# Gate and value products of a feed-forward as 2x2 blocks with seven block products

## The chip, the cores and the metric

One core of one Trainium2 chip runs the whole program once. The metric is the device time of that execution in microseconds; the kernel before has a median of 2009.08 us over three executions (2008.69 to 2012.46).

## The reference

Four layers over 512 tokens of width 1024, in float32. The first two layers are a mixer (three kinds of attention) and a gated feed-forward; the last two are a recurrent layer ("even") and a gated linear attention layer ("odd"). The change touches the feed-forward of the first two layers alone:

```python
D_MODEL, SEQ, DEPTH = 1024, 512, 2
D_FF = -(-(8 * D_MODEL) // (3 * 256)) * 256     # 2816
for l in range(DEPTH):
    ...
    hn = rms_norm(h, ffn_norm[l])
    gu = hn @ w_gate_up[l]
    h = h + (jax.nn.silu(gu[..., :D_FF]) * gu[..., D_FF:]) @ w_down[l]
```

## The kernel before, in words

Activations lie feature-major: eight tiles of 128 features x 512 tokens. A matmul's float32 operands are each split in two, hi (rounded to the matmul's format) and lo (what is left), and a product is three matmuls into one bank, hi x hi, hi x lo, lo x hi (`mm3`). Weights arrive as units of 128x1024 (512 KB): `wunit` (L316) loads one into a `wr` tile, ScalarE writes `wh`, VectorE writes `wl` as the difference. There are two `wr`, three `wh` and three `wl` buffers; this work has a raised priority, so that it runs ahead of what is next in the program. The rest is ordered by a static planner by priority and program order, each engine then running its queue in order. `evac` takes a product out of PSUM with a multiplication, also at raised priority.

`ffn` (L1276) first calls `prenorm` (L558), which makes the split activations `xs` (`xh`, `xl`) of h times the norm's weight, and `RB`, the reciprocal root mean square of each token spread over all partitions (`RH` is half of it). Then it goes over NF = 22 blocks of 128 hidden columns in groups of 8, 8 and 6. For each block: a gate product (`dense_fm`: 8 k-tiles x 3 = 24 matmuls of 512 columns), taken out as `fz` times RB, tanh on ScalarE into `fth`, a scalar_tensor_tensor on VectorE, then the value product (24 more), taken out as `fth` times RH, their product, and its split into `fah`, `fal`. This is called the gate stage below. Behind each group comes the down stage: for eight outputs a unit of `wd` and 24 (or 18) matmuls over the group's `fah`, `fal`, and an addition into h. PSUM has four tags (pd, pt, pr, pa) of two banks each. Elementwise helpers are `tt` (L285), `stt` (L303), `act` (L306), and the matmul is L366; so lines in the trace are mostly those of helpers, and names of tiles tell operations apart. GpSimd does nothing in the feed-forward. Its few sums stand in the first norm (`acc`) and in the "seam" between the even and the odd layer (`RH`, `sq`, 256 columns).

Of the kernel before, what the change touches and what calls it, by code (L numbers as in the profile page):

```python
# [5 lines left out]
F32 = mybir.dt.float32  # L6
F32R = mybir.dt.float32r
BF16 = mybir.dt.bfloat16
I32 = mybir.dt.int32
AF = mybir.ActivationFunctionType  # L10
ALU = mybir.AluOpType
# [4 lines left out]
P = 128  # L16
T = 512
# [8 lines left out]
UNIT = 1024  # L26
# [12 lines left out]
WPRI, SMPRI, EPRI, CPRI, SPRI = 300, 0, 200, 500, 600  # L39
# [3 lines left out]

WEAVE, VAT, QAT, VDELAY, QAHEAD, RPOST = 1.9, (2, 6, 10, 14), 6, 1, 3, 20
MSCB, MOB, DB0, DB1, DB2 = ("pa", "pr", "pa", "pr"), "pd", ["pd", "pt"], ["pd"], ["pd"]

EARLY, SEAM, LATE, AH2, AH3 = (3, 5), (3, 1, 5, 5, 1), 2, -300, -250

# [170 lines left out]
class _Kernel:  # L219
# [1053 lines left out]
            self.add(self.h[m], ps, self.h[m])  # L1273


    def ffn(self, l):  # L1276
        self.dbanks = ["pd", "pt", "pr"]
        xs, rT, RB, RH = self.prenorm(f"ffn_norm{l}", half=True)
        for k0 in range(0, NF, 8):
            n = min(8, NF - k0)  # L1280
            acts = []
            for m in range(k0, k0 + n):
                pg = self.dense_fm(self.a["wgu"][l, 2 * m], xs)
                z = self.t("fz", "Z")
                self.evac(z, pg, RB)
                th = self.t("fth", "Z")
                self.act(th, z, AF.Tanh, scale=0.5)
                self.stt(z, th, 1.0, z, ALU.add, ALU.mult)
                pu = self.dense_fm(self.a["wgu"][l, 2 * m + 1], xs)
                self.evac(th, pu, RH)  # L1290
                self.mul(z, z, th)
                acts.append(self.split(z, "fa", "F"))
            for m in range(KD):
                ps = self.pd()
                self.dense(ps, self.wunit(self.a["wd"][l, m, :, k0 * P:(k0 + n) * P], n * P), acts)
                self.add(self.h[m], ps, self.h[m])
        if l == 0:
            self.h_kept = self.dr.tile([D, T], F32, tag="hk", name="hk")
        for m in range(KD):
            if l == 0:  # L1300
                self.nc.sync.dma_start(out=self.h_kept[m * P:(m + 1) * P, :], in_=self.h[m])
# [496 lines left out]
    def run(self):  # L1798
        self.setup()
        for l in range(L2):  # L1800
            with self.phase("attn", R=26, M=15, I=2):
                self.attn(l)
            with self.phase("ffn", F=40, Z=8):
                self.ffn(l)
        self.softplus()
        with self.phase("even", A=16, B=16, D=7, U=3, G=7, W=2):
            self.even()
        with self.phase("odd", Q=8, V=8, G=8, L=8, QS=8, K=8, S=3):
            self.odd()
# [42 lines left out]
```

## Time and profile before

| | us |
|---|---|
| median of three executions | 2009.08 |
| the profiled execution: time | 2010.3 |
| the profiled execution: span, first to last instruction | 2008.5 |
| TensorE, VectorE, ScalarE, GpSimd busy in the span | 1972.3, 1274.5, 808.1, 68.9 |
| granted TensorE clock, mean share | 0.998 |
| a gate stage of 8 blocks, a down stage behind it | 87.0, 43.5 |

The time is the span and 1.8 us around it. Matmuls are pipelined: the duration of one is its latency, and what it costs is the distance from its start to the next one's. VectorE's operations overlap a little in the same way. A busy engine is the bound of a stage only if the others wait for it there.

### The profile page before, as it was taken

What the parts mean: (1) busy time and instruction counts of PE and PEld (TensorE: products, weight loads), DVE (VectorE), ACT (ScalarE), POOL (GpSimd) and SP (SyncE); (2) the same over time, 40 slices, a digit from 0 to 9 for tenths busy, and PEclk for the clock granted to TensorE, in tenths of its full rate; (3) what the DMA queues carried; (4) which work ended last, traced back from release to release, by engine and by line L of the source; (5) the groups of instructions that cost most, each with busy time, mean ns of one, the idle gap of its engine ahead of it and who ended that gap; (6) DMA issues with size and microseconds to landing.
All of it is one profiled execution on the core that took longest, in us unless ns stands there. A gap on an engine that the chain in (4) does not pass through costs nothing.

```text
span 2008.5 us, 25747 instructions
## 1 busy us (share of the span) xinstructions
PE 1972.3 (98%) x10016; PEld 1582.8 (79%) x10016; DVE 1274.5 (63%) x2367; ACT 808.1 (40%) x1323; POOL 68.9 (3%) x116
## 2 busy tenths in 40 slices
PE   8999999999999999999999999999999999999998
PEld 5777678888888877766788888888888888888886
DVE  7874665544535688647555354458988884389665
ACT  6523553322223444336433222234545453347242
POOL 3100000000000201000000000000000000020000
PEclk9999999999999999999999999999999999999999
DMA  5420122332332523212233233323333323222221
GB/s 178 127 69 23 52 85 91 99 94 95 96 103 87 166 85 102 52 33 70 74 95 95 95 97 103 95 86 98 97 94 98 100 90 112 93 72 84 74 84 43
DMA packets 64910, 180.06 MB, mean 90 GB/s; under 512 B 13892, under 2 KB 16740, under 8 KB 64788
## 3 DMA queue, kind: packets, MB, share of 16 engines
q1 hardware_dynamic: 60528, 175.27, 27.9%
q0 software_dynamic: 1808, 2.69, 0.5%
q8 instruction: 79, 1.29, 0.3%
q10 hardware_dynamic: 2452, 0.45, 0.2%
q14 instruction: 43, 0.35, 0.1%
HBM read 172.29 MB, written 6.09 MB: 89 GB/s over the span
## 4 chain that ended last, share of the span: by engine, by line
PE 81%; DVE 9%; issue 4%; ACT 3%; DMA 2%; POOL 1%; SPq 0%; DVEq 0%; ACTq 0%; POOLq 0%
PE pd L366 68%; PE msc L366 2%; PE mo L366 2%; DVE wl L285 2%; PE egate L366 1%; PE ro L366 1%; PE mpt L1169 1%; DVE xinv L285 1%; DVE xprod L285 1%; ACT wh L306 1%; PE bch L366 1%; DVE xl L303 1%; DMA wr<-owout 1%; PE ost L366 0%; DVE h L285 0%
## 5 line engine op out<-in xcount | busy, mean ns | idle before, releaser
L366 PE MATMUL pd<-xh,wh 128*128 128x512 f32 (+1 forms) x1512 | 591.2, 391 | 8.3 <-ACT xh L306 6.1
L306 ACT ACTIVATE wh<-wr 128x1024 fp32r<-128x1024 f32 (+3 forms) x285 | 296.3, 1040 | 746.7 <-PE pd L366 517.2
L366 PE MATMUL pd<-xl,wh 128*128 128x512 f32 (+1 forms) x1512 | 592.4, 392 | 4.3 <-DVE xl L303 4.1
L366 PE MATMUL pd<-xh,wl 128*128 128x512 f32 (+1 forms) x1512 | 590.2, 390 | 0.0
L285 DVE TENSOR_TENSOR wl<-wr,wh 128x1024 fp32r<-128x1024 f32 (+3 forms) x285 | 341.6, 1199 | 98.1 <-ACT wh L306 97.6
L366 PEld LDWEIGHTS pd<-xh,wh 128*128 128x128 f32 (+1 forms) x1512 | 284.2, 188 | 68.2 <-ACT xh L306 6.5
L366 PEld LDWEIGHTS pd<-xl,wh 128*128 128x128 f32 (+1 forms) x1512 | 284.3, 188 | 66.7 <-DVE xl L303 8.4
L366 PEld LDWEIGHTS pd<-xh,wl 128*128 128x128 f32 (+1 forms) x1512 | 284.4, 188 | 57.3 <-issue 1.0
L285 DVE TENSOR_TENSOR h<-pd,h 128x512 f32<-128x512 f32 x64 | 44.2, 691 | 150.1 <-PE pd L366 150.1
L366 PE MATMUL pd<-fal,wh 128*128 128x512 f32 x352 | 137.2, 390 | 0.0
L366 PE MATMUL pd<-fah,wl 128*128 128x512 f32 x352 | 137.0, 389 | 0.0
L366 PE MATMUL pd<-fah,wh 128*128 128x512 f32 x352 | 136.7, 389 | 0.0
L285 DVE TENSOR_TENSOR fth<-pd,RH 128x512 f32<-128x512 f32 x44 | 30.4, 692 | 118.6 <-PE pd L366 118.6
L366 PE MATMUL pd<-mxh,wh 128*128 128x512 f32 (+1 forms) x272 | 102.8, 378 | 0.0
L366 PE MATMUL pd<-mxh,wl 128*128 128x512 f32 (+1 forms) x272 | 102.6, 377 | 0.0
L366 PE MATMUL pd<-mxl,wh 128*128 128x512 f32 (+1 forms) x272 | 102.5, 377 | 0.0
L285 DVE TENSOR_TENSOR fz<-pd,RB 128x512 f32<-128x512 f32 x44 | 30.4, 692 | 99.3 <-PE pd L366 99.3
L366 PEld LDWEIGHTS pd<-fal,wh 128*128 128x128 f32 x352 | 66.1, 188 | 14.4 <-DVE fal L285 0.7
L366 PEld LDWEIGHTS pd<-fah,wh 128*128 128x128 f32 x352 | 66.0, 188 | 14.0 <-ACT fah L306 0.3
L366 PEld LDWEIGHTS pd<-fah,wl 128*128 128x128 f32 x352 | 66.1, 188 | 13.7
L366 PEld LDWEIGHTS pd<-mxh,wl 128*128 128x128 f32 x272 | 51.2, 188 | 9.3
L366 PEld LDWEIGHTS pd<-mxl,wh 128*128 128x128 f32 x272 | 51.2, 188 | 9.3
(509 smaller groups left out, 2851.4 us busy)
## 6 DMA issues: line engine op xcount, KB each, us to landing
wr<-wgu SPq DMA_DIRECT2D x88, 512.0 KB, 3.5
wr<-ewin SPq DMA_DIRECT2D x48, 512.0 KB, 3.5
wr<-win SPq DMA_DIRECT2D x35, 512.0 KB, 3.6
wr<-wd SPq DMA_DIRECT2D x32, 512.0 KB, 3.5
wr<-wout SPq DMA_DIRECT2D x16, 512.0 KB, 3.5
wr<-ewout SPq DMA_DIRECT2D x16, 512.0 KB, 3.8
wr<-wd SPq DMA_DIRECT2D x16, 384.0 KB, 3.2
h<-xT SPq DMA_DIRECT2D x16, 256.0 KB, 4.9
```

The costliest lines, as they stand in the source:

```text
L285: (eng or self.nc.vector).tensor_tensor(out, x, y, op)
L303: (eng or self.nc.vector).scalar_tensor_tensor(out=out, in0=x, scalar=s, in1=y, op0=op0, op1=op1)
L306: self.nc.scalar.activation(out, x, f, **kw)
L366: self.nc.tensor.matmul(out=out, lhsT=lhsT, rhs=rhs, start=start, stop=stop)
L1169: nc.tensor.transpose(ps[:, qb * P:qb * P + P], prs[qb][:, kb * P:kb * P + P], self.ident)
```

## The change

Each block's gate and value products are taken as one product of a 2x2 block matrix with another. The weight matrix has rows gate and value, split over k in two halves (k-tiles 0 to 3 and 4 to 7): a11, a12 (gate), a21, a22 (value). The activations are split over k in the same halves and over tokens in two of 256: b11, b12, b21, b22. Seven block products (Winograd's form of Strassen's) take the place of eight: a11 b11, a12 b21, (a11-a21) t3, a22 t4, s1 t1, s2 t2, s4 b22, with s1 = a21+a22, s2 = s1-a11, s4 = a12-s2 and t1 to t4 differences of the b's. Each is 4 k-tiles x 3 matmuls of 256 columns.

`halves` makes t1 to t4 once a layer: it forms h times the norm's weight again in float32 on ScalarE, four differences of 256 columns for each of four k pairs (two on VectorE, two on GpSimd), and splits them. `gate_up` replaces the body of the loop for blocks 2 to 21 (PLAIN = 2): it loads the gate unit into its own buffer `fg` and the value unit into `wr`, does four sums of 512 columns on GpSimd (into one buffer `fs` and, for a11-a21, in place), splits the gate unit, the value unit (its first half now a11-a21), s1, and s2 with s4 as one unit. After the products it combines the four banks A, B, C, E into the gate and value halves: a copy on ScalarE and four additions on VectorE that read PSUM, at evac's priority; multiplication with RB and RH, tanh, the scalar_tensor_tensor, the product and the split follow. The buffers of the stage become F=19, W=4 instead of F=40, Z=8.

```diff
--- before.py
+++ after.py
@@ -43,6 +43,8 @@
 
 WEAVE, VAT, QAT, VDELAY, QAHEAD, RPOST = 1.9, (2, 6, 10, 14), 6, 1, 3, 20
 MSCB, MOB, DB0, DB1, DB2 = ("pa", "pr", "pa", "pr"), "pd", ["pd", "pt"], ["pd"], ["pd"]
+
+PLAIN = 2
 
 EARLY, SEAM, LATE, AH2, AH3 = (3, 5), (3, 1, 5, 5, 1), 2, -300, -250
 
@@ -1273,17 +1275,107 @@
             self.add(self.h[m], ps, self.h[m])
 
 
+    def halves(self, gname):
+
+
+        out, H = [], T // 2
+        for j in range(4):
+            x = []
+            for k in (j, j + 4):
+                t = self.t("fx", "F")
+                self.act(t, self.h[k], AF.Copy, scale=self.vc(gname, k))
+                x.append(t)
+            t = [self.t("ft", "F") for _ in range(2)]
+            b11, b12, b21, b22 = (x[i][:, c:c + H] for i in range(2) for c in (0, H))
+            t1, t2, t3, t4 = (t[i][:, c:c + H] for i in range(2) for c in (0, H))
+            self.sub(t1, b12, b11)
+            self.sub(t3, b22, b12, self.nc.gpsimd)
+            self.sub(t2, b22, t1)
+            self.sub(t4, b21, t2, self.nc.gpsimd)
+            hi, lo = (self.php.tile([P, UNIT], F32R, tag=f"T{n}{j}", name=n, bufs=1) for n in ("th", "tl"))
+            for i in range(2):
+                c = slice(i * T, i * T + T)
+                self.act(hi[:, c], t[i])
+                self.sub(lo[:, c], t[i], hi[:, c].bitcast(F32))
+            out.append([(hi[:, i * H:i * H + H], lo[:, i * H:i * H + H]) for i in range(4)])
+        return out
+
+    def gate_up(self, l, m, xs, ts, RB, RH):
+
+        nc, H, pool = self.nc, T // 2, self.nc.gpsimd
+        g = self.php.tile([P, UNIT], F32, tag="fg", name="fg", bufs=2)
+        u = self.wp.tile([P, UNIT], F32, tag="wr", name="wr", bufs=2)
+        S = self.php.tile([P, 3 * T], F32, tag="fs", name="fs", bufs=1)
+        s1, s2, s4 = (S[:, i * T:i * T + T] for i in range(3))
+        a11, a12, a21, a22 = (x[:, c:c + T] for x in (g, u) for c in (0, T))
+
+        def unit(x):
+            hi = self.wp.tile([P, UNIT], F32R, tag="wh", name="wh")
+            lo = self.wp.tile([P, UNIT], F32R, tag="wl", name="wl")
+            self.act(hi, x)
+            self.sub(lo, x, hi.bitcast(F32))
+            return hi, lo
+
+        with self.tc.high_priority(WPRI):
+            nc.sync.dma_start(out=g, in_=self.a["wgu"][l, 2 * m])
+            nc.sync.dma_start(out=u, in_=self.a["wgu"][l, 2 * m + 1])
+            self.add(s1, a21, a22, pool)
+            self.sub(a21, a11, a21, pool)
+            self.sub(s2, s1, a11, pool)
+            self.sub(s4, a12, s2, pool)
+            wg, wu, w1 = unit(g), unit(u), self.split(s1, "f1", "W")
+            ws = unit(S[:, T:])
+        A, B, C, E = self.pt("fA"), self.pr("fB"), self.pa("fC"), self.bank("pd", "fE")
+
+        def product(ps, w, o, x):
+            for j in range(4):
+                c = slice(o + j * P, o + j * P + P)
+                self.mm3(ps, (w[0][:, c], w[1][:, c]), x[j], j == 0, j == 3)
+
+        lo, hi = slice(0, H), slice(H, T)
+        b11, b21, b22 = ([(xs[k + j][0][:, c], xs[k + j][1][:, c]) for j in range(4)] for k, c in ((0, lo), (4, lo), (4, hi)))
+        t1, t2, t3, t4 = ([ts[j][i] for j in range(4)] for i in range(4))
+        product(A[:, lo], wg, 0, b11)
+        product(B[:, hi], wg, T, b21)
+        product(A[:, hi], wu, 0, t3)
+        product(C[:, hi], wu, T, t4)
+        product(E[:, lo], w1, 0, t1)
+        product(B[:, lo], ws, 0, t2)
+        product(C[:, lo], ws, T, b22)
+        y = self.php.tile([P, 6, H], F32, tag="fy", name="fy", bufs=2)
+
+        def two(x):
+            return x.unsqueeze(1).to_broadcast([P, 2, H])
+
+        with self.tc.high_priority(EPRI):
+            self.act(y[:, 3], A[:, lo])
+            self.add(y[:, 0:3:2], B[:].rearrange("p (s t) -> p s t", t=H), two(y[:, 3]))
+            self.add(y[:, 1], y[:, 0], A[:, hi])
+            self.add(y[:, 0:6:5], y[:, 0:2], two(E[:, lo]))
+            self.add(y[:, 3:5], y[:, 0:2], C[:].rearrange("p (s t) -> p s t", t=H))
+        th, z, up = (y[:, i:i + 2].rearrange("p s t -> p (s t)") for i in (0, 2, 4))
+        self.mul(z, z, RB)
+        self.act(th, z, AF.Tanh, scale=0.5)
+        self.stt(z, th, 1.0, z, ALU.add, ALU.mult)
+        self.mul(up, up, RH)
+        self.mul(z, z, up)
+        return self.split(z, "fa", "F")
+
     def ffn(self, l):
         self.dbanks = ["pd", "pt", "pr"]
         xs, rT, RB, RH = self.prenorm(f"ffn_norm{l}", half=True)
+        ts = self.halves(f"ffn_norm{l}")
         for k0 in range(0, NF, 8):
             n = min(8, NF - k0)
             acts = []
             for m in range(k0, k0 + n):
+                if m >= PLAIN:
+                    acts.append(self.gate_up(l, m, xs, ts, RB, RH))
+                    continue
                 pg = self.dense_fm(self.a["wgu"][l, 2 * m], xs)
-                z = self.t("fz", "Z")
+                y = self.php.tile([P, 6, T // 2], F32, tag="fy", name="fy", bufs=2)
+                th, z = (y[:, i:i + 2].rearrange("p s t -> p (s t)") for i in (0, 2))
                 self.evac(z, pg, RB)
-                th = self.t("fth", "Z")
                 self.act(th, z, AF.Tanh, scale=0.5)
                 self.stt(z, th, 1.0, z, ALU.add, ALU.mult)
                 pu = self.dense_fm(self.a["wgu"][l, 2 * m + 1], xs)
@@ -1800,7 +1892,7 @@
         for l in range(L2):
             with self.phase("attn", R=26, M=15, I=2):
                 self.attn(l)
-            with self.phase("ffn", F=40, Z=8):
+            with self.phase("ffn", F=19, W=4):
                 self.ffn(l)
         self.softplus()
         with self.phase("even", A=16, B=16, D=7, U=3, G=7, W=2):
```

## Rows read from the trace of the kernel before

**Rows 1.** the page's first part: each engine's busy us, share, instructions

```profile
PE 1972.3 (98%) x10016; PEld 1582.8 (79%) x10016; DVE 1274.5 (63%) x2367; ACT 808.1 (40%) x1323; POOL 68.9 (3%) x116
```

**Rows 2.** windows: us, busy (x) of PE, PEld, DVE, ACT, POOL, clock, DMA

```profile
460.90:547.90 87.00, 87.00 (x385) 72.09 (x384) 43.91 (x54) 25.55 (x31) 0.00 (x0) 1.00 0.30 97
547.90:591.40 43.50, 43.50 (x193) 36.03 (x192) 16.54 (x18) 9.13 (x9) 0.00 (x0) 1.00 0.32 97
591.40:656.70 65.30, 65.30 (x289) 54.09 (x289) 32.20 (x40) 18.71 (x23) 0.00 (x0) 1.00 0.30 89
```

**Rows 3.** chain of waits, from 440 to 600 us: start, us, what

```profile
439.98 160.03 PE pd L366 x706
```

**Rows 4.** timeline of PE, gate stage: start us, us, instruction

```profile
519.83 0.39 PE L366 MATMUL pd<-xh,wl 128*128 128x512 f32 x1
...
521.41 0.39 PE L366 MATMUL pd<-xh,wh 128*128 128x512 f32 x1
```

**Rows 5.** timeline of PE and its loads, matmuls of 256 columns

```profile
1749.16 0.28 PE L366 MATMUL pd<-mxh,wl 128*128 128x256 f32 x1
...
1750.12 0.28 PE L366 MATMUL pd<-mxl,wh 128*128 128x256 f32 x1
1749.17 0.19 PEld L366 LDWEIGHTS pd<-mxh,wh 128*128 128x128 f32 x1
```

**Rows 6.** timeline of DVE, gate stage

```profile
482.85 0.69 DVE L285 TENSOR_TENSOR fth<-pd,RH 128x512 f32<-128x512 f32 x1 [2.69 <-PE pd L366]
483.58 0.69 DVE L285 TENSOR_TENSOR fz<-fz,fth 128x512 f32<-128x512 f32 x1
484.19 1.22 DVE L285 TENSOR_TENSOR wl<-wr,wh 128x1024 fp32r<-128x1024 f32 x1
485.32 0.68 DVE L285 TENSOR_TENSOR fal<-fz,fah 128x512 fp32r<-128x512 f32 x1
```

**Rows 7.** timeline of DVE, seam, operations of 256 columns

```profile
1761.75 0.47 DVE L303 SCALAR_TENSOR_TENSOR ey<-ey,vec,spread 128x256 f32<-128x256 f32 x1
1762.14 0.68 DVE L303 SCALAR_TENSOR_TENSOR xl<-h,vec,xh 128x256 fp32r<-128x256 f32 x1
1762.74 0.41 DVE L285 TENSOR_TENSOR h<-h,ey 128x256 f32<-128x256 f32 x1
```

**Rows 8.** groups by line and shape, ACT, gate stage 460.9 to 547.9

```profile
L306 ACT ACTIVATE wh<-wr 128x1024 fp32r<-128x1024 f32 x16 | 17.0, 1062 | 58.0 <-PE pd L366 34.8 <-issue 23.2
L306 ACT ACTIVATE fth<-fz 128x512 f32<-128x512 f32 x8 | 4.9, 616 | 0.0
```

**Rows 9.** timeline of POOL, first norm

```profile
9.22 1.33 POOL L285 TENSOR_TENSOR acc<-acc,sq 128x512 f32<-128x512 f32 x1 [6.18 <-ACT sq L306]
11.98 1.41 POOL L285 TENSOR_TENSOR acc<-acc,sq 128x512 f32<-128x512 f32 x1 [1.44 <-ACT sq L306]
15.18 1.77 POOL L285 TENSOR_TENSOR acc<-acc,sq 128x512 f32<-128x512 f32 x1
```

**Rows 10.** timeline of DVE: one alone, then those beside the first norm's sums

```profile
330.78 0.74 DVE L303 SCALAR_TENSOR_TENSOR xl<-h,vec,xh 128x512 fp32r<-128x512 f32 x1
...
9.79 1.31 DVE L303 SCALAR_TENSOR_TENSOR xl<-h,vec,xh 128x512 fp32r<-128x512 f32 x1 [0.38 <-ACT xh L306]
...
12.16 1.79 DVE L303 SCALAR_TENSOR_TENSOR xl<-h,vec,xh 128x512 fp32r<-128x512 f32 x1
...
15.13 0.69 DVE L285 TENSOR_TENSOR sq<-h 128x512 f32<-128x512 f32 x1 [1.18 <-POOL acc L285]
15.74 1.76 DVE L303 SCALAR_TENSOR_TENSOR xl<-h,vec,xh 128x512 fp32r<-128x512 f32 x1
```

**Rows 11.** timeline of POOL, seam

```profile
1761.81 0.73 POOL L285 TENSOR_TENSOR RH<-RH,sq 128x256 f32<-128x256 f32 x1 [0.39 <-ACT sq L306]
```

**Rows 12.** windows, seam: columns as in rows 2

```profile
1752.20:1756.00 3.80, 2.09 (x16) 1.64 (x15) 2.71 (x11) 2.14 (x4) 0.00 (x0) 0.97 0.37 106
1756.00:1759.20 3.20, 3.20 (x16) 3.20 (x17) 3.20 (x13) 1.45 (x4) 0.99 (x1) 0.50 0.02 5
```

## The prediction

> **What bounds the kernel now.** First the page's first part: TensorE is busy for 98% of the span, VectorE for 63%, GpSimd for 3% [rows 1]. A mean over stages says little, so next come the windows by stage. The feed-forward of a layer alternates gate stages (blocks of 128 hidden columns, in groups of 8, 8 and 6) with down stages (eight outputs each). A gate stage of 8 blocks lasts 87.0 us, one of 6 lasts 65.3 us, both 10.87 us a block, with TensorE busy throughout at granted clock 1.00. VectorE is busy for 43.9 of the 87.0 us, and for only 16.5 of the 43.5 us of a down stage [rows 2]. The chain of waits is one unbroken piece of matmuls there [rows 3]. So TensorE bounds these stages, and a block is worth what its matmuls cost: 48 of 512 columns, one each 0.226 us (seven steps from 519.83 to 521.41) [rows 4]. What other engines do is free as long as it fits into 10.87 us a block. That is the point that decides this change.
>
> **TensorE's part.** A changed block has 7 products x 4 k-tiles x 3 terms = 84 matmuls of 256 columns, 7/8 of the columns. The trace has such matmuls, each with its own 128x128 load, at full clock: eight steps from 1749.16 to 1750.12, 0.120 us each [rows 5]. That is more than half of 0.226, so part of the gain is lost: 84 x 0.119 (between 0.117 and 0.121) = 10.0 us a block, 0.87 us less than now. Over 40 blocks (20 a layer, the first two stay as they are) TensorE alone would give 35 us. The weight load, recorded at 0.19 us, is longer than the 0.120 us step and yet doesn't set it [rows 5]: loads overlap matmuls and each other. The Trainium skill speaks against this (TensorE: Matmul & The Clock Gate, Part 3, The mechanism): loads overlap running matmuls only when the row group differs, which it doesn't here; by that rule the change would lose on TensorE itself. The row disagrees, so the sum goes by the row.
>
> **VectorE's part, the term that decides.** Now: two weight splits and five operations of 512 columns, 43.9 / 8 = 5.5 us a block. After: three splits of 1024 columns (gate, value, and s2 with s4), one of 512 (s1), four combinations that read PSUM (three of 512, one of 256), then z*RB, up*RH, the stt, the product and the split's difference. Steps from start to start: 1.13 us for 1024 columns (484.19 to 485.32), 0.61 for 512, 0.73 where the next operation reads the result (482.85 to 483.58) [rows 6]; for 256 columns 0.41 less the 0.08 by which neighbours overlap, 0.34 [rows 6, 7]. Sum: 3 x 1.13 + 0.61 (s1) + 0.73 + 0.46 + 0.61 + 0.73 (PSUM, in a chain) + 0.61 + 0.61 + 0.73 + 0.61 + 0.61 = 9.7 us. So VectorE alone goes from half idle to 97% of TensorE's 10.0 us. ScalarE has 3 x 1.06 + 4 operations of 0.62 at most = 5.7 us [rows 8]; it stays free. DMA moves the same bytes.
>
> **GpSimd's part.** Four sums of 512 columns a block, each with two SBUF inputs. The trace has four like it: at 9.22, 1.33 us; one that began at 15.18 while a VectorE sum ran (15.13 to 15.82) and ended at 16.95, that is 1.13 us after it [rows 9, 10]. So one costs about 1.13 us by itself, 4.5 us a block, which GpSimd can afford. What matters is what VectorE does meanwhile: an xl operation lasts 0.74 us alone, but 1.31, 1.79 and 1.76 us beside these sums, ending 0.55 us after the sum each time (11.10 after 10.55, 13.95 after 13.40, 17.50 after 16.95) [rows 9, 10]. The extra is 0.57, 1.05, 1.02: mean **0.88 us a collision**. An operation that reads one input from PSUM is untouched (0.47 us at 1761.75 beside the sum of 1761.81), the next one, with both inputs in SBUF, is held (0.68 us at 1762.14) [rows 7, 11]. The Trainium skill states the same kind of lock (SBUF — State Buffer, Who interferes with whom), but for the whole instruction. By that each sum would cost VectorE 1.13 us and the block 9.7 + 4.5 = 14.2; the three rows show less, because a waiting operation has its start-up behind it, so the sum goes by 0.88. The bounds are 0 (all hidden) and 1.14; nothing lets a sum make VectorE faster, so no gain.
>
> How many of the four collide? The buffer of the sums exists once, so a block's s1 can start only when the block before has split s2 and s4, and that split waits for a weight buffer which is free only at the end of a block's products. So the four start behind that split; what VectorE has ready then is up*RH, the stt, the product, the final difference and the next block's two weight splits, all with both inputs in SBUF. The PSUM combinations come later or are just done. I take all four: **9.7 + 4 x 0.88 = 13.2 us a block**, VectorE-bound, TensorE idle for 3.2 of them.
>
> **The sum.** A group gets a credit, because VectorE has 27 us idle in the down stage ahead [rows 2]: the first block's gate, value and s1 splits (2.9) and its four sums (3.5) are done there; at the end the down stage's first 21 matmuls (4.7 us) don't need the last block, less two down-weight splits (2.3) and ScalarE's step (0.6): 1.8. Together 8.2 us.
> Group of 8: 8 x 13.2 - 8.2 = 97.4 against 87.0: +10.4. Group of 6: 79.2 - 8.2 = 71.0 against 65.3: +5.7.
> First group (2 plain, 6 changed): +5.7 and the new `halves`: on VectorE 8 differences of 256 and 8 of 512, 8 x 0.34 + 8 x 0.61 = 7.6 us, and 8 GpSimd sums of 256 columns (0.73 us each [rows 11]), at the same ratio, 0.88 of 1.13, up to 0.57 each on VectorE, 4.5. ScalarE's 16 more are covered. Cover is two plain blocks: 21.7 us, of which VectorE now uses 11.0. 11.0 + 7.6 + 4.5 + the first changed block's 6.4 = 29.5, 7.8 too many; between 0 and 8 I take 5, as the first product needs only the gate split. +10.7.
> A layer: 10.4 + 5.7 + 10.7 = 26.8; two layers +53.6. The profiled execution has a span of 2008.5 and a time of 2010.3 us; the median shown is 2009.1, so its stages stand for the median within 0.1%. Forecast: 2009.1 + 53.6 = **2062.7 us**.
> With c as the cost of one sum, break-even lies near 11.8 us a block (a group of 8: 8 x 11.8 - 7 = 87): c = 0.53, or 2.4 full collisions of four.
> Bounds of the forecast's mechanism: c at 0.6 gives 12.1 us a block and some +16 us, 2025; c at 1.14 with 0.5 us of VectorE idling in its queue gives 14.8, credit 9.3: 22.1 + 14.2 + 22.2 a layer, 2126.
>
> **Rivals.**
> *The sums hide* (ends faster). They run beside the 2.5 us of PSUM combinations and beside idle time, two or fewer collide, and TensorE stays the bound. Then 40 x -0.87 = -35, back 0 to 5 a layer for `halves` and up to 2.4 at six group ends (the last combination chain of 4.8 us no longer fits ahead of matmul 21): 1974 to 1995, say **1984**. For it: rows show that PSUM operations pass, and the PSUM combinations of a block are one after the other. Against: the order argued above, and that without any collision VectorE has only 0.3 us a block to spare. It decides from c under 0.53. Chance 0.21.
> *The clock falls.* In the seam, after 3.8 us with TensorE busy for 2.09, it ran at granted clock 0.50, the level of 1.2 GHz, for 3.2 us; in the gate stages, never idle, it stays at 1.00 [rows 2, 12]. If the 3.2 idle us a block come in one piece and the clock is halved for most of a block, 84 matmuls cost nearly 20 us and TensorE is the bound again, 40 x 4 or more above now: **2170 and up**. A short fall is hidden behind VectorE. Chance 0.06.
> *Loads don't hide.* Were the step set by the load (0.19 us), a block would be 84 x 0.19 = 16 us, 40 x 5.1 = +205: **2214**. The 0.120 us steps deny it [rows 5]. This is the rule of the Trainium skill named above (TensorE: Matmul & The Clock Gate), taken as a mechanism. Chance 0.01.
>
> **How the numbers follow.** VectorE-bound 0.72, sums hidden 0.21, clock 0.06, loads 0.01. Of the 0.72, 0.04 lies within 0.2% (4 us, about what a measurement of this kernel can tell from no change) and 0.03 below it. Faster 0.24, same 0.04, slower 0.72. The range reaches from the hidden case's inner part to c = 1.14: 1982 to 2126; the likeliest case's own range is 2025 to 2126.
>
> **What would show it.** In a gate stage: 256-column matmuls 0.119 us apart where they flow (right for TensorE); VectorE over 90% busy, TensorE near 76%; about 12 to 13 us a changed block; the stt, product, split rows at means of 1.0 to 1.6 us where they are 0.69 or 1.22 now; GpSimd sums at 1.3 to 1.8 us; TensorE's waits put down to VectorE's weight splits. The down stages stay at 43.5 us. It is wrong if VectorE's rows keep their lengths (no collisions), if TensorE stays over 97% busy (hidden), or if the granted clock leaves 1.00.

## The result, and the profile after

The changed kernel takes 2119.83 us (median of four runs, 2117.58 to 2120.12) against 2010.47 for the kernel before (median of four): ratio 1.0541 [1.0523, 1.0559], 109 us slower. The forecast was 2062.7, so the direction and the engine that binds were right, and the size was half of what came.

The page's first part of the kernel after, to be laid beside [rows 1]:

```profile
span 2115.8 us, 29450 instructions
PE 1991.2 (94%) x11456; PEld 1663.7 (79%) x11456; DVE 1604.7 (76%) x2639; ACT 902.7 (43%) x1479; POOL 364.6 (17%) x292
```

VectorE is busy for 330 us more, GpSimd for 296 us more. TensorE's busy time also grew, by 19 us, although it multiplies 7/8 of the columns in 40 blocks. In part that is the clock: the mean granted clock of the span is 0.977.

The windows by stage of layer 0, after (columns as in [rows 2]): first six changed blocks, down stage, group of 8, group of 6:

```profile
360.60:434.50 73.90, 66.20 (x505) 65.18 (x504) 71.34 (x70) 29.30 (x40) 36.25 (x20) 0.93 0.23 74
434.50:482.20 47.70, 45.49 (x194) 37.14 (x194) 23.98 (x27) 10.45 (x12) 6.44 (x4) 0.96 0.34 107
482.20:584.90 102.70, 89.04 (x674) 87.09 (x673) 98.75 (x94) 38.55 (x53) 49.35 (x28) 0.93 0.23 74
632.60:707.20 74.60, 66.60 (x506) 65.31 (x506) 71.04 (x69) 28.20 (x39) 35.07 (x20) 0.93 0.18 58
```

The column to read is DVE: 98.75 of 102.70 us, against 43.91 of 87.00 in [rows 2]. VectorE is the bound of every gate stage, and TensorE now waits there (89.04 of 102.70). The down stage grew too, from 43.5 to 47.7 us, which the prediction had excluded.

Where the time is, by stage (span after less span before, each stage from its first matmul to that of the next; the first line runs from the layer's first gate matmul, at 328.71 after and 328.57 before, to the first changed block, at 360.56 after and, in the old kernel, six blocks of 10.87 us ahead of its end of stage, near 352.2):

| stage of layer 0 | before, us | after, us | difference | forecast |
|---|---|---|---|---|
| norm, `halves`, two plain blocks | 23.6 | 31.9 | +8.3 | +5 |
| six changed blocks | 65.2 | 74.0 | +8.8 | +5.7 |
| down stage | 43.5 | 47.7 | +4.1 | 0 |
| group of 8 | 87.0 | 102.7 | +15.7 | +10.4 |
| down stage | 43.5 | 47.8 | +4.2 | 0 |
| group of 6 | 65.3 | 74.6 | +9.3 | +5.7 |
| last down stage | 33.1 | 34.7 | +1.6 | 0 |
| layer 0 (unrounded) | | | +51.9 | +26.8 |

The spans differ by 2115.8 - 2008.5 = 107.3 us, so 55.4 are left. Layer 1 shows the same pattern and takes 51.2 of them: +7.7, +7.2, +5.5, +14.2, +5.5, +9.3 and +1.9 in the order of the table. The other 4.2 lie outside the two feed-forwards.

A steady block of the group of 8, and how it differs from the first ones: window of the third block, then of the fourth to fifth, once the pace has changed:

```profile
502.40:513.00 10.60, 10.35 (x87) 10.14 (x86) 10.39 (x12) 3.60 (x6) 3.73 (x3) 1.00 0.32 100
517.60:531.70 14.10, 10.59 (x87) 10.19 (x85) 13.89 (x14) 5.01 (x7) 7.14 (x4) 1.00 0.23 76
```

The blocks start at 482.21, 492.28, 502.36, 512.94, 527.03, 542.63, 556.72 and 570.83: 10.08 us each for the first two and 10.6 for the third, while VectorE lives on what it did in the down stage ahead, then 14.1 (one of 15.6). In the later stretch VectorE is busy for 13.89 of 14.10 us. The chain of waits from 517 to 532 us has one summary by line; VectorE is the only engine in it, and "issue" stands for time in which the profile shows no wait:

```profile
by line: DVE fy L287 32.5%; DVE wl L287 23.6%; DVE fy L305 22.8%; DVE f1l L287 11.3%; issue 10.9%; DVE fal L287 4.0%; DVEq L287 0.1%
```

Now the timeline of VectorE in that stretch, some operations left out (start, us, instruction):

```profile
518.11 0.69 DVE L287 TENSOR_TENSOR fy<-fy 128x512 f32<-128x512 f32 x1
518.72 1.22 DVE L287 TENSOR_TENSOR wl<-wr,wh 128x1024 fp32r<-128x1024 f32 x1
...
523.02 1.22 DVE L287 TENSOR_TENSOR wl<-fs,wh 128x1024 fp32r<-128x1024 f32 x1
524.16 0.68 DVE L287 TENSOR_TENSOR fy<-fy,RB 128x512 f32<-128x512 f32 x1
524.76 1.78 DVE L287 TENSOR_TENSOR fy<-fy,RH 128x512 f32<-128x512 f32 x1
526.47 2.30 DVE L287 TENSOR_TENSOR wl<-fg,wh 128x1024 fp32r<-128x1024 f32 x1
528.69 1.77 DVE L287 TENSOR_TENSOR f1l<-fs,f1h 128x512 fp32r<-128x512 f32 x1
530.39 1.77 DVE L305 SCALAR_TENSOR_TENSOR fy<-fy 128x512 f32<-128x512 f32 x1
```

The timeline of GpSimd beside it:

```profile
524.32 1.67 POOL L287 TENSOR_TENSOR fs<-wr 128x512 f32<-128x512 f32 x1 [6.80 <-DVE wl L287]
526.07 1.62 POOL L287 TENSOR_TENSOR wr<-fg,wr 128x512 f32<-128x512 f32 x1
527.65 2.27 POOL L287 TENSOR_TENSOR fs<-fs,fg 128x512 f32<-128x512 f32 x1
530.00 1.62 POOL L287 TENSOR_TENSOR fs<-fg,fs 128x512 f32<-128x512 f32 x1
```

The first sum waits 6.80 us for the split of `fs` (523.02), as the prediction argued from the single buffer. From then on the two engines take turns: VectorE's operation is recorded longer by 1.78 - 0.69 = 1.09, 2.30 - 1.22 = 1.08, 1.77 - 0.69 = 1.08 and 1.77 - 0.69 = 1.08 us, once for each sum. Four such steps are 4.3 us; the block of 14.1 less these is 9.7, the very sum the prediction made for VectorE without collisions. So the count of operations and of collisions was right, and the price of a collision was not: 1.09 us, not 0.88.

### The profile page after: what moved, and what is told of

Its sections match the earlier page's. It is cut to its first block, busy times and chain, and to the rows that moved or that the text cites. A ratio compares the mean times of both kernels' runs of the same rounds, so it can differ in the third digit from the quotient of the medians.

```text
span 2115.8 us, 29450 instructions
## 1 busy us (share of the span) xinstructions
PE 1991.2 (94%) x11456; PEld 1663.7 (79%) x11456; DVE 1604.7 (76%) x2639; ACT 902.7 (43%) x1479; POOL 364.6 (17%) x292
## 4 chain that ended last, share of the span: by engine, by line
PE 56%; DVE 28%; issue 9%; ACT 3%; POOL 2%; DMA 1%; DVEq 0%; SPq 0%; ACTq 0%; POOLq 0%
PE pd L368 42%; DVE wl L287 8%; DVE fy L287 8%; DVE fy L305 3%; DVE f1l L287 2%; PE msc L368 1%; PE mo L368 1%; PE egate L368 1%; PE fA L368 1%; PE ro L368 1%; PE fC L368 1%; DVE fal L287 1%; DVE xprod L287 1%; DVE xinv L287 1%; PE oo L368 1%
## 5 line engine op out<-in xcount | busy, mean ns | idle before, releaser
L368 PE MATMUL pd<-xh,wh 128*128 128x512 f32 (+1 forms) x872 | 344.0, 395 | 8.6 <-ACT xh L308 7.0
L368 PE MATMUL pd<-xl,wh 128*128 128x512 f32 (+1 forms) x872 | 344.2, 395 | 4.1 <-DVE xl L305 3.9
L368 PE MATMUL pd<-xh,wl 128*128 128x512 f32 (+1 forms) x872 | 342.5, 393 | 0.0
L368 PEld LDWEIGHTS pd<-xh,wh 128*128 128x128 f32 (+1 forms) x872 | 165.3, 190 | 43.8 <-ACT xh L308 7.0
L368 PEld LDWEIGHTS pd<-xl,wh 128*128 128x128 f32 (+1 forms) x872 | 164.9, 189 | 41.6 <-DVE xl L305 7.7
L368 PEld LDWEIGHTS pd<-xh,wl 128*128 128x128 f32 (+1 forms) x872 | 164.9, 189 | 32.8 <-issue 1.0
L287 POOL TENSOR_TENSOR fs<-wr 128x512 f32<-128x512 f32 x40 | 64.0, 1600 | 419.1 <-DVE wl L287 221.0
L368 PE MATMUL fA<-th,wl 128*128 128x256 f32 x160 | 54.0, 338 | 47.8 <-DVE wl L287 47.8
L287 DVE TENSOR_TENSOR wl<-fg,wh 128x1024 fp32r<-128x1024 f32 x40 | 86.2, 2154 | 3.2 <-ACT wh L308 3.2
L287 POOL TENSOR_TENSOR fs<-fs,fg 128x512 f32<-128x512 f32 x40 | 85.6, 2140 | 0.0
```

The lines of the kernel that those rows point to most:

```text
L287: (eng or self.nc.vector).tensor_tensor(out, x, y, op)
L368: self.nc.tensor.matmul(out=out, lhsT=lhsT, rhs=rhs, start=start, stop=stop)
```

## The experiments

Kernel times given without an interval are of a single execution. The theory that went into these experiments: the four sums on GpSimd hold VectorE's operations whose inputs are both in SBUF, 1.09 us each, and this makes the block 14.1 us. The rivals: the cost is latency (the single buffer of the sums makes them late), or the sums' own work wherever it is done, or something else in the changed block (256-column matmuls, the clock).

### The sums on VectorE

```diff
-        nc, H, pool = self.nc, T // 2, self.nc.gpsimd
+        nc, H, pool = self.nc, T // 2, self.nc.vector
```

> The four sums of weights of each changed block run on VectorE instead of GpSimd; nothing else changes. Theory (port lock: in the changed kernel each sum holds up a VectorE operation for 1.09 us, 1.78 less 0.69): the four lock delays of 4.4 us a block go, four operations of 0.61 to 0.73 us come, 2.6 us: 12.3 us a block in the middle of a gate stage instead of 14.1, all VectorE rows back to 0.69 and 1.22 us, time near 2060 us (2050 to 2075). Rival (the sums are on the path because they are slow and wait for one buffer, 1.6 to 2.3 us each on GpSimd): the sums now take 0.7 us each, so the block would fall to what TensorE needs, 10 to 11 us, time under 2020 us.

Measured: 2002.84 us, ratio 0.9958 [0.9928, 0.9989] against before. The same work on the busier engine makes the kernel 117 us faster than with GpSimd's help, and the expected 2050 to 2075 was too high. Groups of VectorE by shape, 490 to 560 us:

```profile
L287 DVE TENSOR_TENSOR wl<-fg,wh 128x1024 fp32r<-128x1024 f32 x4 | 4.9, 1218 | 0.2 <-ACT wh L308 0.2
L287 DVE TENSOR_TENSOR fy<-fy,RH 128x512 f32<-128x512 f32 x7 | 4.8, 682 | 0.0
L287 DVE TENSOR_TENSOR fs<-fs,fg 128x512 f32<-128x512 f32 x4 | 2.7, 682 | 0.0
```

Every operation has its own length back, and a sum on VectorE is recorded at 682 ns, 0.60 us from start to start, little more than half of what it cost VectorE from GpSimd. A block then asks VectorE for 3 x 1.14 + 13 x 0.60 + 0.33 = 11.6 us without gaps. That is just under the break-even of 11.8 that the prediction had worked out with the credit ahead of a group. Windows of the group of 8, its first five blocks and the other three:

```profile
459.40:509.80 50.40, 50.40 (x421) 50.37 (x420) 48.41 (x68) 22.45 (x29) 0.00 (x0) 1.00 0.27 86
509.80:545.50 35.70, 32.25 (x254) 31.85 (x253) 33.81 (x50) 14.93 (x20) 0.00 (x0) 0.95 0.32 106
```

Five blocks run at TensorE's pace, 10.08 us each; only the sixth and seventh take longer (11.9 and 13.8). I had expected the old gaps between VectorE's operations to stay beside the new work; the sums fill them. Nor had I counted that the down stages return to 43.8 and 43.7 us. The rival "it is the work itself" falls, and so does "256-column matmuls": they flow at 50.40 / 420 = 0.120 us each.

### Writes without sums

Each sum is replaced by two fills with zeros of the same buffer, on GpSimd (the weights of four products are then not the reference's).

```diff
-            self.add(s1, a21, a22, pool)
-            self.sub(a21, a11, a21, pool)
-            self.sub(s2, s1, a11, pool)
-            self.sub(s4, a12, s2, pool)
+            for x in (s1, a21, s2, s4):
+                for _ in range(2):
+                    pool.memset(x, 0.0)
```

> Each of the four sums is replaced by two fills with zero on GpSimd into the same place: GpSimd stays busy, with the same buffers and waits, but reads nothing (the products are then not the reference's). Theory (the lock is about reading): VectorE's rows go back to 0.69 and 1.22 us although GpSimd works beside them, VectorE needs 9.7 us a block, TensorE 10.0 is the bound, time 1980 to 2000 us. Rival (any GpSimd work beside VectorE holds it up, or GpSimd's length is what counts): rows of VectorE stay long, or blocks stay near 13 us, time over 2080 us.

Measured: 1991.1 us, as expected. Window of the whole group of 8:

```profile
460.70:541.30 80.60, 80.60 (x673) 80.59 (x672) 73.17 (x99) 40.26 (x54) 29.46 (x60) 1.00 0.34 100
```

GpSimd's fills and a VectorE split beside them, groups by shape:

```profile
L1324 POOL MEMSET fs<- 128x512 f32 x42 | 20.5, 527 | 13.8 <-DVE wl L287 13.4
L287 DVE TENSOR_TENSOR wl<-fg,wh 128x1024 fp32r<-128x1024 f32 x6 | 7.3, 1221 | 0.6 <-ACT wh L308 0.6
```

All eight blocks take 10.08 us with the same buffers, order and waits. GpSimd is busy for 29.46 us here, yet the split keeps its 1.22 us. So GpSimd being busy isn't the cause by itself: sums that read SBUF hold VectorE, fills that only write it don't. Whether it is the reading or something else in which a sum differs from a fill, this run doesn't separate. On the latency of the buffer it says less, as the eight fills of a block are shorter than its four sums (29.46 against 49.35 us in the group); against that rival stands the kernel after itself, where VectorE is busy for 13.89 of 14.10 us, while a late buffer would leave it idle. VectorE's busy time here is 73.17 / 8 = 9.15 us a block (the first block's splits lie ahead of the window).

### Half of each sum

Sums over 256 of the 512 columns (the other halves are left as they were; `fs`, now allocated once a layer, is set to zero at its start, which isn't shown in the cut).

```diff
-            self.add(s1, a21, a22, pool)
+            c = slice(0, H)
+            self.add(s1[:, c], a21[:, c], a22[:, c], pool)
```

(the other three sums likewise)

> The sums are done over half of their columns, 256 instead of 512 (the other half is left at what it was, so the result is not the reference's). Theory (the delay is the length of the sum on its port): a sum of 256 columns takes 0.73 us by itself in the kernel before, 0.4 less than one of 512, so a collision costs about 0.7 instead of 1.09 us; a block 9.7 + 2.8 = 12.5 us, time 2060 to 2075 us. Rival (a collision costs a fixed hand-over, whatever the size): 14.1 us a block, time within 10 us of 2120.

Measured: 2033.26 us, below the expected 2060 to 2075. Timeline of VectorE:

```profile
516.12 0.68 DVE L287 TENSOR_TENSOR fy<-fy,fC 128x512 f32<-128x512 f32 x1
...
517.49 1.23 DVE L287 TENSOR_TENSOR fy<-fy,RH 128x512 f32<-128x512 f32 x1
518.64 1.76 DVE L287 TENSOR_TENSOR wl<-fg,wh 128x1024 fp32r<-128x1024 f32 x1
520.33 1.22 DVE L305 SCALAR_TENSOR_TENSOR fy<-fy 128x512 f32<-128x512 f32 x1
```

The timeline of GpSimd beside it:

```profile
516.28 0.74 POOL L287 TENSOR_TENSOR fs<-fs,fg 128x256 f32<-128x256 f32 x1 [6.78 <-DVE wl L287]
517.10 1.07 POOL L287 TENSOR_TENSOR fs<-fg,fs 128x256 f32<-128x256 f32 x1
```

A collision costs 1.23 - 0.69 = 0.54, 1.76 - 1.22 = 0.54 and 1.22 - 0.69 = 0.53 us, half of 1.09: between these two sizes the price is in proportion to the sum's columns. The expectation had kept four collisions; only three happened, since the first sum (516.28) ran beside the combination with `fC` in PSUM, which kept its 0.68. This block is 11.49 us, near 9.7 + 3 x 0.54 = 11.3; the first five of the group take 10.08 each.

### An own buffer for s1

s1 gets two buffers of its own, so that it needn't wait for the split of s2 and s4. (For the room the stage has F=18 instead of 19; the cut leaves that out, and the split's new argument.)

```diff
-        S = self.php.tile([P, 3 * T], F32, tag="fs", name="fs", bufs=1)
-        s1, s2, s4 = (S[:, i * T:i * T + T] for i in range(3))
+        s1 = self.php.tile([P, T], F32, tag="fs1", name="fs1", bufs=2)
+        S = self.php.tile([P, 2 * T], F32, tag="fs", name="fs", bufs=1)
+        s2, s4 = (S[:, i * T:i * T + T] for i in range(2))
```

> s1 gets a buffer of its own, twice, so that the first two sums of a block (s1 and a11-a21, on which the value unit's split waits) need not wait for the split of s2 and s4 of the block before. The buffer F of the stage gives one of 19 for the room. Theory (VectorE's port is the bound): sums start earlier but still lock VectorE four times a block; 14.1 us a block and 2105 to 2125 us, lower only if a sum falls beside the additions that read PSUM (then 13 us a block, 2075). Rival (the sums' latency and their one buffer are the bound): TensorE's waits for the value unit's split vanish, blocks near 11 us, time under 2050 us.

Measured: 2100.12 us, some 20 below the kernel after and just below the expected 2105 to 2125. Timeline of GpSimd, then of VectorE:

```profile
534.77 1.43 POOL L287 TENSOR_TENSOR fs<-wr 128x512 f32<-128x512 f32 x1 [6.42 <-DMA wr<-wgu]
534.97 0.68 DVE L287 TENSOR_TENSOR fy<-fy,fC 128x512 f32<-128x512 f32 x1
535.68 1.07 DVE L287 TENSOR_TENSOR fy<-fy,RB 128x512 f32<-128x512 f32 x1
```

The sums are still paid: from 522.19 to 535.68, 13.5 us, the operations with RB and RH, the split of `fg` and the stt are longer than their own lengths by 0.40, 1.10, 1.08 and 1.08 us, 3.7 in all instead of 4.3, because the first sum now runs partly beside a combination that reads PSUM. The run is a weak test of the rival "latency": the first sum now waits for the DMA of the value unit, and starts only some 0.3 us ahead of the end of the split of `fs`, where it started 0.1 us behind it.

### Idle sums in the kernel before

The old kernel, with four sums a block on a buffer that nothing reads. In the first form nothing ties them to their block; in the second the first group has none.

```diff
+        dead = self.php.tile([P, UNIT], F32, tag="dead", name="dead", bufs=1)
...
+                with self.tc.high_priority(WPRI):
+                    for i in range(4):
+                        self.add(dead[:, T:], dead[:, :T], dead[:, T:], self.nc.gpsimd)
```

> The kernel before, with four sums of 512 columns added on GpSimd for every block of the gate stage, on a buffer that nothing else reads. Theory (a collision costs VectorE 1.09 us, and that costs time only where VectorE has none to spare): several of VectorE's rows grow from 0.69 or 1.22 us to 1.2 to 2.3, VectorE goes from 5.5 to at most 9.9 us a block, under TensorE's 10.87; gate stages stay at 87.0 and 65.3 us and the time within 6 us of before (a few us in the norm ahead of the first block are possible). Rival (GpSimd's sums delay the path by themselves, through SBUF or through TensorE's reads): gate stages grow by 3 us a block, time over 2080 us.

> The kernel before with four idle sums on GpSimd for every block of the second and third group only, none for the first group, whose sums ran into the norm ahead of it when all blocks had them (first gate stage 11 us later a layer). Theory: with VectorE at under 9.9 of 10.87 us a block the sums cost nothing, time equal to before within 3 us, although VectorE's rows grow. Rival: the collisions cost something by themselves in the gate stages, 5 us or more.

Measured: 2031.67 us, and 2029.4 for the second, ratio 1.0086 [1.0069, 1.0103]. Both miss: I had expected nothing of either. The second one's timeline of GpSimd around the norm ahead of the feed-forward shows why:

```profile
332.21 98.30 POOL L285 TENSOR_TENSOR dead<-dead 128x512 f32<-128x512 f32 x56
```

The timeline of VectorE in that norm, two of its operations:

```profile
340.66 1.12 DVE L300 TENSOR_SCALAR rs_ipre<-rs_wpre 128x4 f32<-128x4 f32 x1
343.36 1.11 DVE L285 TENSOR_TENSOR rs_wpre<-rs_wpre,rs_hpre 128x4 f32<-128x4 f32 x1
```

Nothing paces idle sums, so all 56 of them ran in one piece from the norm on. The norm's operations on 4 columns, 0.16 us long in the kernel before, are held for 1.1 us each, TensorE waits for them, and from the layer's first gate matmul to the unbroken part of the gate stage it takes 14.6 us instead of 7.3, in both layers. The first group then takes 1.9 and 1.1 us longer; together 17.5, where 18 were measured. So these two say little of the blocks, but they price a serial norm under such sums. One of the two operations shown, a TENSOR_SCALAR, reads only one tensor: on four columns, operations with a single input are held too.

### Idle sums, paced

The same, but each idle sum reads its block's own `wh`, so that it can't run before that block; groups 2 and 3 only.

```diff
+                w = self.wunit(self.a["wgu"][l, 2 * m])
+                if k0:
+                    with self.tc.high_priority(WPRI):
+                        for i in range(4):
+                            self.add(dead, w[0][:, :T].bitcast(F32), dead, self.nc.gpsimd)
```

> The kernel before with four idle sums on GpSimd for each block of the second and third group, each reading the block's own split gate unit, so that they can't all run ahead (in the two runs with free idle sums the planner let them run in one stretch from the norm on). Theory: about four collisions of 1.09 us a block, VectorE at 9 to 10 us of 10.87 a block, TensorE still the bound: gate stages of 87.0 and 65.3 us, time within 3 us of before. Rival (sums cost the path something by themselves, SBUF or TensorE's reads): the stages grow by 1 us a block or more, over 2035 us.

Measured: 2011.16 us, ratio 1.0 [0.9991, 1.001], as expected. Window of the group of 8, to be read against the first of [rows 2]:

```profile
464.60:551.60 87.00, 87.00 (x386) 72.06 (x385) 64.50 (x54) 25.57 (x31) 51.44 (x28) 1.00 0.32 99
```

Groups of VectorE by shape in that stage:

```profile
L285 DVE TENSOR_TENSOR wl<-wr,wh 128x1024 fp32r<-128x1024 f32 x16 | 27.0, 1687 | 2.6 <-ACT wh L306 2.6
L285 DVE TENSOR_TENSOR fal<-fz,fah 128x512 fp32r<-128x512 f32 x7 | 11.3, 1619 | 0.0
L285 DVE TENSOR_TENSOR fz<-pd,RB 128x512 f32<-128x512 f32 x8 | 5.5, 692 | 6.2 <-PE pd L366 5.6
```

The same kind of collision, 20.6 us in all (VectorE 64.50 against 43.91 us), in a stage that still lasts 87.00. By 28 sums that is 0.74 us each, less than 1.09, on a VectorE that is not always ready. They are free there, since VectorE has 22 us to spare. Collisions alone don't make a kernel slower; on an engine that has been filled up they do. The operation with PSUM among its inputs keeps 0.69 us, as the prediction read from [rows 7]; this row is the firmer one, since the operation at 1761.75 had begun ahead of the sum at 1761.81.

### Fewer changed blocks

Two forms of the kernel after, with GpSimd's sums: every second block changed, and the last block of each group left plain.

```diff
-                if m >= PLAIN:
+                if m >= PLAIN and m % 2 == 0:
```

> The changed kernel with sums on GpSimd, but only every other block from 2 on in the new form (ten a layer instead of twenty). Theory (VectorE's sum over neighbouring blocks decides): a pair needs 5.5 + 14.1 = 19.6 us of VectorE and 10.87 + 10.08 = 20.95 of TensorE, so TensorE is the bound again in the middle of a group, 20 x -0.79 = -16 us, and the norm ahead gives back up to 8 a layer: 2000 to 2012 us. Rival (each block with sums costs its 3.2 us wherever it stands): half of the 109 us loss stays, about 2065 us.

```diff
-                if m >= PLAIN:
+                if m >= PLAIN and m < k0 + n - 1:
```

> The changed kernel with the last block of each group in the old form (17 changed blocks a layer instead of 20), sums on GpSimd. Theory (part of the loss lies at the group ends: the down stage waits 2.3 us for the last block's split and then runs 3.4 us at half clock, 4.2 us a long down stage): each of the last blocks falls from 14.1 to 10.9 us, and the down stages return to 43.5 to 44.5 us: 6 x 3.2 + 4 x 3.7 + 2 x 1 = 36 us less than 2120, 2084 (2075 to 2092). Rival (the down stages are longer for a reason of their own, their weights): only the blocks' 19 us come back, 2100 us.

Measured: 2017.0 us for the first (expected 2000 to 2012), 2083.3 for the second (as expected). Windows of the first one's group of 8 and the down stage behind it:

```profile
469.30:553.20 83.90, 83.90 (x529) 76.34 (x528) 63.90 (x77) 33.15 (x42) 19.35 (x12) 1.00 0.32 100
553.20:596.70 43.50, 43.50 (x193) 36.02 (x192) 19.09 (x19) 9.77 (x10) 6.45 (x4) 1.00 0.33 99
```

Window of the second one's down stage behind its first group:

```profile
436.40:479.90 43.50, 43.50 (x194) 36.03 (x193) 19.51 (x20) 9.70 (x11) 6.44 (x4) 1.00 0.35 109
```

With every second block plain TensorE never waits in a group (83.90 of 83.90) and the changed blocks save what they were meant to: 83.90 is 3.1 us less than 87.0. Yet the kernel is 5 us slower than before. From the layer's first gate matmul to the first changed block it takes 31.0 and 32.0 us in the two layers instead of 23.6, so 16 us are lost ahead of the groups, and 10 x 2 x 0.8 = 16 gained in them. The norm takes the gain, at the end of what I had allowed for it; the 5 us on top lie outside the feed-forwards, in one execution, and I can't explain them. And with a plain block at the end of each group the down stages are back at 43.5 us: their +4.2 comes from the changed block at the group's end.

### A version that beats both

The sums on VectorE, and one block of the group of 8 (the fifth) left plain, so that VectorE catches up. In a second form the sums of `halves` go to VectorE as well.

```diff
-        nc, H, pool = self.nc, T // 2, self.nc.gpsimd
+        nc, H, pool = self.nc, T // 2, self.nc.vector
...
-                if m >= PLAIN:
+                if m >= PLAIN and m != 12:
```

> Sums on VectorE as in the run with that change, and block 12 (the fifth of the middle group) by the old form. In that run only the last two blocks of the middle group fell behind TensorE's 10.08 us, by 5.6 us together a layer, because VectorE needs about 11.7 us a block and its backlog had reached the banks. Theory: a plain block (VectorE 5.5 us, TensorE 10.87) clears the backlog: all blocks of the group at TensorE's pace, 5.6 less 0.8 us saved a layer, 1993 us (1989 to 1998). Rival (the two slow blocks come from the end of the group, its first down weights): the loss stays, about 2004 us.

> As the kernel with block 12 plain, and also the eight differences of 256 columns a layer that halves has on GpSimd run on VectorE. Theory: the small operations of the norm's reciprocal root (128x4) were held up to 0.7 us each by those differences; they go back to 0.16 us, the first changed block starts 1 to 4 us earlier a layer, 1987 to 1993 us. Rival: VectorE's 2.7 us more a layer in the cover of the two plain blocks cancel it, no change within 3 us.

Measured: 1991.6 us, ratio **0.9898 [0.9883, 0.9913]**, and 1991.91, ratio 0.9899 [0.9882, 0.9915]. Windows of the first form: group of 8, group of 6:

```profile
460.00:541.40 81.40, 81.40 (x637) 79.51 (x636) 79.12 (x112) 37.28 (x49) 0.00 (x0) 1.00 0.32 99
585.00:645.50 60.50, 60.50 (x506) 60.48 (x505) 58.44 (x83) 26.84 (x36) 0.00 (x0) 1.00 0.26 79
```

TensorE is busy for all of both stages at granted clock 1.00, and VectorE for 79.12 of 81.40 us: both are full. Against 87.0 and 65.3 that is 5.6 and 4.8 us less, and with 4.7 of the first six blocks, less 1.8 ahead of them (25.4 us from the layer's first gate matmul, 23.6 before) and 0.4 in the down stages, 13 a layer and 26 in all; 20.5 were measured, the rest lies outside the feed-forwards. In the second form those 25.4 us are 23.3, 2.0 less, and the first group is 63.1 us long instead of 60.5. The expected gain of that form did not come, its rival did: the sums of `halves` may stand on either engine.

## Why the prediction was right in its way and wrong in its size

**TensorE's part: right.** 84 matmuls of 256 columns take 10.08 us wherever VectorE keeps up, 0.120 each; 10.0 was forecast. By the Trainium skill's rule on loads (TensorE: Matmul & The Clock Gate, Part 3, The mechanism) they would have cost more; the rows of the sums on VectorE, 420 loads and matmuls in 50.40 us, disagree with it, as [rows 5] did.

**VectorE without collisions: right.** 9.7 us forecast; 14.1 - 4 x 1.09 = 9.7 in the block shown, 9.15 of busy time in the run with fills.

**Which operations collide: right.** Four in each block, between the split of `fs` and the next block's operations; combinations out of PSUM pass.

**The price of a collision: the step that failed in the sum.** The prediction averaged three rows of the first norm, 0.57, 1.05 and 1.02 us [rows 9, 10], to 0.88. The first of these came 0.57 us into a sum that was already running (the xl at 9.79 beside the sum of 9.22), so it waited only for the rest of one. It is a partial collision, which happens when VectorE is half idle. In a stage where VectorE is always ready the two engines alternate, and each operation waits for a whole sum: 1.09. Leaving the partial row out would have given 1.035. The reason given for a price below the sum's own 1.13, a start-up that a waiting operation has behind it, leaves no more than 1.13 - 1.09 = 0.04 us. The Trainium skill's rule (SBUF — State Buffer, Who interferes with whom) is the lock for the whole instruction, which the prediction priced at 14.2 us a block and set aside; the measured 14.1 agrees with it. With 1.09 the prediction's own formula gives 8 x 14.1 - 8.2 = 104.6 for the group of 8 and 76.4 for six, against 102.7 and 74.0 to 74.6 measured: the credit was some 2 us too small. Price and credit together are 12.0 of the 25.1 us that were missing in layer 0 (15.7 + 9.3 + 8.8 measured, 21.8 forecast).

**The norm ahead: taken from the middle of its bounds, and it lay at the end.** The forecast had 5 us of 0 to 8 for `halves`; layer 0 shows 8.3. What was left out: the first changed block's four sums carry raised priority and need only its weights, so GpSimd runs them in the norm. Timeline of VectorE after:

```profile
341.44 1.23 DVE L305 SCALAR_TENSOR_TENSOR rs_ypre<-rs_ipre,rs_ypre 128x4 f32<-128x4 f32 x1
343.19 1.22 DVE L287 TENSOR_TENSOR rs_wpre<-rs_ypre 128x4 f32<-128x4 f32 x1
346.13 0.15 DVE L305 SCALAR_TENSOR_TENSOR rs_ypre<-rs_wpre,rs_ypre 128x4 f32<-128x4 f32 x1
```

The timeline of GpSimd beside it:

```profile
340.40 2.25 POOL L287 TENSOR_TENSOR fs<-fs,fg 128x512 f32<-128x512 f32 x1
342.73 1.66 POOL L287 TENSOR_TENSOR fs<-fg,fs 128x512 f32<-128x512 f32 x1
```

The norm's 4-column operations, 0.15 us by themselves, take 1.2 beside the sums. With the blocks' sums on VectorE it takes 25.4 us from the layer's first gate matmul to the first changed block instead of 31.9: 6.5 of the 8.3 us are these sums (and the kernel before, with idle sums, lost 7.3 in the same place). Some 2 of the 6.5 are the clock: TensorE had been waiting for the norm (busy for 0.21 of the 4.11 us up to 344.1), and its granted clock is 0.50 from 344.1 to 350.9, while it stays at 1.00 there with the sums on VectorE. The other 1.8 are `halves`; with its sums on VectorE too, the 23.3 us are those of the kernel before.

**The down stages: excluded, and +4.2 each.** "The down stages stay at 43.5 us" was the second step that failed, 9.9 us in layer 0. The credit assumed that the last block's output comes before matmul 21 of the down stage; with VectorE's queue late it doesn't. TensorE's timeline after, in the second down stage:

```profile
593.26 0.79 PE L368 MATMUL pd<-fah,wh 128*128 128x512 f32 x1 [2.31 <-ACT fah L308]
```

Two windows on both sides of that wait's end (columns as in [rows 2]):

```profile
589.85:593.26 3.41, 1.09 (x6) 0.57 (x4) 2.53 (x5) 1.26 (x2) 0.00 (x0) 1.00 0.50 154
593.28:596.69 3.41, 3.41 (x8) 2.73 (x9) 1.55 (x3) 1.06 (x1) 0.00 (x0) 0.50 0.00 0
```

TensorE waits 2.31 us for the last `fah`. In the 3.41 us before the matmul at 593.26 it was busy for 1.09, and in the 3.41 us after it the granted clock is 0.50, the level of 1.2 GHz: eight matmuls instead of fifteen, 47.7 x (1 - 0.96) = 1.9 us. Both together are the 4.2. A plain block at the end of each group removes them.

**The rivals.** *The sums hide* did not happen with GpSimd; its time, 1984, is near what came of the fills (1991.1) and of the sums on VectorE with one plain block (1991.6). *The clock falls* did happen, for stretches of 3.4 us (0.93 over a gate stage), but in the gate stages they lie beside VectorE's queue. The block of 15.6 us (527.03 to 542.63) shows it: from 535.3 to 538.7 its matmuls run at granted clock 0.50, which makes it 1.5 longer, while VectorE's multiplications with RB go on every 14.1 us (524.16, 538.25, 552.34). They cost at the group ends and, for 6.8 us, behind the norm. *Loads don't hide* did not happen.

TensorE's share in a gate stage was forecast near 76% and is 87% (89.04 / 102.7). That doesn't contradict VectorE as the bound: matmuls at half clock are recorded as busy for twice as long, and the first three blocks flow.

What stays open: why the kernels with changed blocks lose some us outside the two feed-forwards (4.2 in the kernel after), and what in a sum, beside its reading of SBUF, could hold VectorE where a fill doesn't.

## What to carry to other kernels

An engine that goes from half idle to full is the price of such a change; count its operations by start-to-start steps, and then what other engines' operations take from it, at the price of a full collision, because waits seen while the engine was half idle can be partial and too small. Work handed to GpSimd was no help to VectorE when both inputs are in SBUF: in a stage that VectorE bounds, a sum cost it 1.09 us from there and 0.60 when it did it itself. When an algebraic saving fills a second engine, a mix of new and old blocks (here one plain block of eight) lets it catch up and keeps the saving, and work without a consumer nearby needs something that paces it, or it lands on a serial stage such as a norm.

## What was not expected of the hardware

A collision costs VectorE time in proportion to the columns of GpSimd's sum (0.54 us for 256, 1.09 for 512) whatever VectorE's own operation is, 512 or 1024 columns. Operations of VectorE on four columns are held as well, 0.15 to 1.2 us, among them a TENSOR_SCALAR with one input. GpSimd's fills, 0.53 us of writes each, held nothing. And a wait of 2.3 us of TensorE is paid nearly twice: the granted clock was 0.50 for the 3.41 us that followed it.
